# Column products with standing weights and joined high and low inputs in a hybrid encoder block

## The chip, the cores and the metric

The kernel runs on one core of one Trainium2 chip. The metric is the device time of one execution in microseconds (us). Of the kernel before, three runs gave a median of 793.23 us (792.94 to 793.36). The profile is that of one further execution; its times count from the start of its span.

The engines are called as in the profile: PE (TensorE: products; PEld is its loading of weights), DVE (VectorE), ACT (ScalarE), POOL (GpSimd) and SP (SyncE, whose queue starts the weights' transfers).

## The reference

One layer of an encoder on x of 256 tokens by 1024 features, in float32. Five residual parts follow one another:

```python
x = x + 0.5 * rmsnorm(swiglu(rmsnorm(x), w_in, w_down))      # FFN 1, width 2816
h = rmsnorm(x)
q_a, f_a, i_a, g_a, q_b, k_b, v_b, f_b, gates = split(h @ w_in)
A = hgrn2_chunkwise(q_a, f_a, i_a)      # gated linear recurrence, 8 heads of 128
B = fox_attention(q_b, k_b, v_b, f_b)   # causal attention with forget gates
y = sigmoid(gate_A) * (A @ w_branch_a) + sigmoid(gate_B) * (B @ w_branch_b)
x = x + rmsnorm(y @ w_out)
x = x + rmsnorm(mem_cross_attention(rmsnorm(x), rmsnorm(mem)))   # 4 heads, 256 memory rows
x = x + 0.5 * rmsnorm(swiglu(rmsnorm(x), w_in2, w_down2))    # FFN 2
```

with `swiglu(h) = (silu(gate) * up) @ w_down`, where `gate` and `up` are the two halves of `h @ w_in`, and `rmsnorm` dividing each token by the root of its mean square. The kernel applies that per-token factor (`rstd`) after the product, and the gain of each feature before it.

## The kernel before, in words

**Numbers in two parts.** A float32 number is split into a high part that TensorE takes in one pass (`F32R`) and the low rest. A product is three: high by high, high by low, low by high, summed in PSUM. Weights come as units of 512 KB, [128 x 1024], through SP's queue into `raw` (four buffers); ACT casts `hi` (L142) and DVE subtracts to `lo` (L144), eight buffers each. A `chunk` (L153) is four units: 1024 rows of 512 columns, in eight blocks `kb` of 128 rows.

**Two forms of projection.** `proj_tok` (L184): 128 tokens stand in the array and the weights move, 512 columns wide; 24 products for each half of the tokens. The result has tokens on the partitions. `proj_col` and `proj_col2` (L193, L202): a 128x128 block of weights stands and the 256 tokens move, 24 products of 256 for 128 columns: weight high by input high, the same by input low, weight low by input high. The result has features on the partitions, which is what a following product needs. The inputs lie in a `Pair` (L166), with high and low parts in different tiles.

**The feed-forwards** (`ffn`, L352) run over 11 chunks of 256 gate and 256 up columns. A chunk is done in token form (`act_tok`, L382): two halves, each with Silu on ACT (L372, with the token's factor as a scale) and the product with `up` on DVE (L377). For the down product its result has to have features on the partitions: `flush` (L358) issues four transposes on PE (L367) behind a given product, and splits their result (L162, L163). `down` (L401) then adds the chunk's 24 products of 512 columns to four accumulators. The first chunks go differently: in the first feed-forward chunks 0 to 2 walk through both token halves at once (`act_first`, L387), as the inputs arrive; in the second, chunks 0 and 1 are taken half by half while the residual before is finished (`second_half`, L418). The down products trail the chunks by one or two; the last three chunks (`STAG`) are left to the end, where `post` (L310) or `post_last` (L325) normalises the sum and adds it to `xs`: squares summed on ACT (L250), the product with the gain on DVE (L317, L340), the factor from `rstd_of` (L227).

**Around the change.** The per-token factors as a row over all partitions come from `row_of` (L270): DVE transposes, a POOL transfer to DRAM, and a POOL transfer back to all partitions (L275, L277). Forget gates (L575 to L588) and the recurrence's queries (L589 to L599) are column products, then multiplied by that row (L581, L596). Memory queries (L1047 to L1053) are column products that `split` brings into high and low. They are followed by the memory values (`mem_v`) and the scores (`mem_scores`, L1071). `half` (L524) transposes the new `xs` for the next part's input.

**The order** is that of the program, with two changes: `after(i)` gives a group priority behind the i-th product that was issued (constants such as `L_ACT`), and the scheduler of the framework moves instructions of an engine where it expects an operand later. PSUM has eight banks: four `acc`, two `mm`, two `tr`.

Of the kernel before, what the change touches and what calls it, by code (L numbers as in the profile page):

```python
# [18 lines left out]
P = 128  # L19
# [16 lines left out]
L_ACT = 21  # L36
L_LAST = 8
L_F1 = 24
# [41 lines left out]
def block_kernel(ctx: ExitStack, tc: tile.TileContext, wts, head_in, gf_in, x_in, mem_in, memT_in, cols, rows, fbias, masks, out):  # L80
# [85 lines left out]
    class Pair:  # L166
# [14 lines left out]
        def lo(self, kb, a=0, b=T):  # L181
            return self.l[kb // 4][:, kb % 4, a:b]

    def proj_tok(ps, X, units, h, n=512):  # L184
# [63 lines left out]

    def ssq(dst, src):
        S.activation(junk[:, : src.shape[-1]], src, AF.Square, accum_out=dst)  # L250

# [7 lines left out]

    fac = [cp.tile([P, 64], F32, name=nm("fac")) for _ in range(2)]  # L260
    for t in fac:
# [47 lines left out]

    def post(ps, h, grow, factor=1.0, store=False):  # L310

        s = s1(2, name="ss2")
        ts = []
        for j in range(2):
            ssq(s[:, j : j + 1], ps[j])
            t = sp.tile([P, 512], F32, tag="z2", name=nm("post"), bufs=3)
            V.scalar_tensor_tensor(out=t, in0=ps[j], scalar=-factor * SC_RSTD, in1=grow[:, j * 512 : (j + 1) * 512], op0=ALU.mult, op1=ALU.mult)  # L317
            ts.append(t)
        r = rstd_of(s, scaled=False)
        for j, (t, xh) in enumerate(zip(ts, x_halves(h))):  # L320
            V.scalar_tensor_tensor(out=xh, in0=t, scalar=r, in1=xh, op0=ALU.mult, op1=ALU.add)
            if store:
                nc.sync.dma_start(out[h * P : (h + 1) * P, j * 512 : (j + 1) * 512], xh)

    def post_last(ps, h, grow, factor):  # L325

        s = s1(2, name="ss2")
        ts = []
        for j in range(2):
            ssq(s[:, j : j + 1], ps[j])  # L330
# [9 lines left out]
            V.scalar_tensor_tensor(out=t, in0=ps[j], scalar=-factor * 16.0, in1=grow[:, j * 512 : (j + 1) * 512], op0=ALU.mult, op1=ALU.mult)  # L340
            ts.append(t)
# [9 lines left out]

    def ffn(w_in, w_dn, X, r2, n_tok, i_row, first_half, second_half=None):  # L352

        acts = {}
# [15 lines left out]
        def act_evac(ps, c, h):  # L370
            sg = sp.tile([P, FC], F32, tag="c1", name=nm("sg"), bufs=7)
            silu = S.activation(sg, ps[:, :FC], AF.Silu, scale=r2[h])  # L372
            if c == NFF - 1 and h == 1 and not first_half:
                with tc.issue_after(silu.ins):
                    S.activation(warm, ones[:, 0:1], AF.Abs_reciprocal_sqrt)
            a = sp.tile([P, FC], F32, tag="c1", name=nm("at"), bufs=7)
            V.scalar_tensor_tensor(out=a, in0=ps[:, FC:], scalar=r2[h], in1=sg, op0=ALU.mult, op1=ALU.mult)  # L377
            ats[c, h] = a
            if h == 1:
                late.append(c)  # L380

        def act_tok(c, h):  # L382
            ps = mm()
            proj_tok(ps, X, chunk(w_in, c), h)
            act_evac(ps, c, h)

        def act_first(cs, bank):  # L387
# [25 lines left out]
        for h in range(2):  # L413
            m = len(log)
            for c in range(n_tok):
                act_tok(c, h)
            if h == 0 and n_tok:
                second_half(m)  # L418
        accs = None
        done = 0  # L420
        if callable(r2):
            outs = act_first((0, 1), acc)
            r2 = r2()
            for c in range(2):
                acts[c] = m4([P, 2, 2, T], F32R, "act")
# [3 lines left out]
        for c in range(n_tok, NFF):  # L429
# [28 lines left out]
        for cut in (left, right):  # L458
            for c in range(NFF - STAG, NFF):
                if c == NFF - 1 and cut == left:  # L460
                    flush(m + L_LAST)
                down(c, 0, (cut,))
        post(accs[0], 0, grow, 0.5, not first_half)
        m = len(log)
        if first_half:
            for c in range(NFF - STAG, NFF):
                down(c, 1)
            first_half(m)
            post(accs[1], 1, grow, 0.5)
        else:  # L470
            for cut in (left, right):
                for c in range(NFF - STAG, NFF):
                    down(c, 1, (cut,))
            post_last(accs[1], 1, grow, 0.5)

    X1 = Pair()
    heads, raw1 = [], []  # L480
# [31 lines left out]
    def norm_1():  # L512
# [6 lines left out]
        return [rstd_x(x_halves(h)) for h in range(2)]  # L519

    X2 = Pair()
    r2 = [None, None]
# [46 lines left out]

    def halves(ps):  # L570
        return ps.rearrange("p h (b t) -> p h b t", b=2)
# [17 lines left out]
    for c in range(2):  # L589
        u = chunk("q_a", c)  # L590
        q = m4([P, 2, 4, P], n="q")
        for j in range(2):
            qj = heads_of(q, j)
            ps = proj_col2(X2, u, (2 * j, 2 * j + 1))
            z = sp.tile([P, 2, 2, P], F32, tag="z2", name=nm("z2"), bufs=3)
            V.tensor_tensor(out=z, in0=halves(ps), in1=bc(row2h, [P, 2, 2, P], 1), op=ALU.mult)  # L596
            S.activation(qj, z, AF.Sigmoid)
# [420 lines left out]

    X3 = Pair()
    r3 = [None, None]  # L1020
# [111 lines left out]
    for kb in range(4):  # L1132
        behind.extend(marks[kb // 2])
        unit("mo", kb)
        behind.clear()
    X4 = Pair()
    r4 = [None, None]
# [8 lines left out]
    rows_proj(po[1], AO, "mo", 1, range(3, KB))  # L1146
    half(X4, r4, 0, G_F2, m + L_MO)
    post(po[1], 1, g3)


    def second(m):
        half(X4, r4, 1, G_F2, m + L_F2)

# [92 lines left out]
```

## Time and profile before

| | |
|---|---|
| median of three runs | 793.23 us |
| lowest and highest | 792.94, 793.36 us |
| the profiled execution | 791.78 us |
| its span | 790.0 us |
| its granted TensorE clock | 0.998 |
| weights and other data moved | 147.82 MB, mean 187 GB/s |
| PE instructions in the span | 4736 products and transposes |
| transposes of flushes (L367) | 22 x 4 |

How to read the profile's lines. In the page's list of busy times, each engine has its busy time, its share of the span and its number of instructions. A line of a group gives the line of the source, the engine, the operation, output and inputs by tile name, the shapes and the count, then the busy time and the mean duration of one in ns, then the time that the engine was idle just before and what ended it. A line of a timeline begins with its start and its duration. Products on PE overlap in the record: the time of one in a row of many is the distance between starts. A line of windows has, for each engine, the busy time in a stretch and the number of instructions.

### The profile page before, as it was taken

Reading aid. Unit: us, or ns where it says so; the run is one execution under the profiler, and the core shown is the slowest. Engines: PE = TensorE matmul, PEld = TensorE weight load, DVE = VectorE, ACT = ScalarE, POOL = GpSimd, SP = SyncE. Lnnn points to the kernel's source line nnn. Section 1 sums busy time; section 2 is a strip of 40 time slices with the busy share of each in tenths; the row PEclk is TensorE's granted clock in tenths of the full one; section 3 lists DMA queues with packets and bytes.
Section 4 is the critical chain, followed back from the end, with each engine's and each line's share of the span. In section 5 each row is a group of like instructions: output and inputs, shape, how many; then the busy total and the mean of one; then the engine's idle time right before and its main releaser. Section 6 shows DMA issues by size and latency. Waiting matters only on the chain.

```text
span 790.0 us, 12203 instructions
## 1 busy us (share of the span) xinstructions
PE 782.3 (99%) x4736; PEld 677.4 (86%) x4736; DVE 519.0 (66%) x825; ACT 426.8 (54%) x656; POOL 13.7 (2%) x36
## 2 busy tenths in 40 slices
PE   9999999999999999999999999999999999999996
PEld 7888888888899999998788888999888888888885
DVE  6774545557767899488686666964669754545543
ACT  7654444546664677357774345643657644434541
POOL 0000000000000102100000000000000000000000
PEclk9999999999999999999999999999999999999999
DMA  9786654563654547634576654555263655554521
GB/s 347 247 271 205 228 189 160 188 202 118 210 196 144 180 136 224 258 120 152 197 251 222 211 191 160 164 186 181 65 229 134 227 199 209 203 200 161 183 84 54
DMA packets 44345, 147.82 MB, mean 187 GB/s; under 512 B 5048, under 2 KB 8768, under 8 KB 44288
## 3 DMA queue, kind: packets, MB, share of 16 engines
q1 hardware_dynamic: 43168, 144.83, 53.9%
q0 software_dynamic: 688, 1.85, 1.0%
q8 instruction: 37, 0.61, 0.3%
q10 hardware_dynamic: 432, 0.37, 0.1%
q14 instruction: 20, 0.16, 0.1%
HBM read 145.97 MB, written 1.06 MB: 186 GB/s over the span
## 4 chain that ended last, share of the span: by engine, by line
PE 98%; DMA 1%; DVE 0%; ACT 0%; SPq 0%; issue 0%; DVEq 0%; ACTq 0%
PE mm L94 68%; PE acc L94 27%; PE tr L367 1%; PE tr L94 1%; PE tr L294 1%; DMA head<-in_head_dram 1%; PE tr L898 0%; PE tr L989 0%; PE acc L1099 0%; DVE xs L348 0%; DVE post L340 0%; ACT hi L507 0%; SPq L491 0%; ACT hT L285 0%; SPq L486 0%
## 5 line engine op out<-in xcount | busy, mean ns | idle before, releaser
L144 DVE TENSOR_TENSOR lo<-raw,hi 128x1024 fp32r<-128x1024 f32 (+1 forms) x256 | 306.7, 1206 | 122.4 <-ACT hi L142 114.3
L142 ACT CAST hi<-raw 128x1024 fp32r<-128x1024 f32 (+1 forms) x256 | 262.4, 1038 | 149.3 <-PE mm L94 83.3
L94 PE MATMUL mm<-lo,hT 128*128 128x512 f32 (+1 forms) x592 | 226.9, 385 | 0.0
L94 PE MATMUL mm<-hi,hT 128*128 128x512 f32 (+1 forms) x592 | 226.8, 385 | 0.0
L94 PE MATMUL mm<-hi,lT 128*128 128x512 f32 (+1 forms) x592 | 226.5, 385 | 0.0
L94 PEld LDWEIGHTS mm<-hi,lT 128*128 128x128 f32 x592 | 111.2, 188 | 21.4 <-DVE lT L286 0.2
L94 PEld LDWEIGHTS mm<-hi,hT 128*128 128x128 f32 x592 | 111.2, 188 | 21.4 <-ACT hT L285 0.3
L94 PEld LDWEIGHTS mm<-lo,hT 128*128 128x128 f32 x592 | 111.0, 188 | 20.7
L94 PE MATMUL acc<-hi,act 128*128 128x512 f32 x352 | 111.8, 390 | 0.0
L94 PE MATMUL mm<-hT,lo 128*128 128x256 f32 x384 | 109.0, 284 | 0.0
L94 PE MATMUL mm<-hT,hi 128*128 128x256 f32 x384 | 108.9, 284 | 0.0
L94 PE MATMUL mm<-lT,hi 128*128 128x256 f32 x384 | 108.8, 283 | 0.0
L94 PEld LDWEIGHTS acc<-hi,act 128*128 128x128 f32 x352 | 66.0, 188 | 13.6 <-DVE act L163 0.4
L94 PEld LDWEIGHTS mm<-hT,hi 128*128 128x128 f32 x384 | 73.6, 192 | 0.1
L94 PEld LDWEIGHTS mm<-lT,hi 128*128 128x128 f32 x384 | 73.6, 192 | 0.1
L94 PEld LDWEIGHTS mm<-hT,lo 128*128 128x128 f32 x384 | 73.6, 192 | 0.1
L94 PE MATMUL acc<-lo,act 128*128 128x512 f32 x176 | 69.7, 398 | 0.0
L372 ACT ACTIVATE sg<-mm,rstd 128x256 f32<-128x256 f32 x40 | 19.0, 475 | 75.8 <-PE mm L94 75.8
L377 DVE SCALAR_TENSOR_TENSOR at<-mm,rstd,sg 128x256 f32<-128x256 f32 x40 | 19.2, 481 | 57.4 <-ACT sg L372 57.4
L94 PEld LDWEIGHTS acc<-lo,act 128*128 128x128 f32 x176 | 33.1, 188 | 6.1
L94 PE MATMUL acc<-hi,hT 128*128 128x512 f32 x96 | 35.0, 392 | 0.5 <-ACT hi L507 0.4
L94 PE MATMUL acc<-hi,lT 128*128 128x512 f32 x96 | 35.1, 393 | 0.0
(198 smaller groups left out, 655.7 us busy)
## 6 DMA issues: line engine op xcount, KB each, us to landing
raw<-in_wts_dram SPq DMA_DIRECT2D x247, 512.0 KB, 4.4
raw<-in_gf_dram SPq DMA_DIRECT2D x12, 344.0 KB, 3.8
head<-in_head_dram SPq DMA_DIRECT2D x7, 392.0 KB, 6.6
grow<-in_rows_dram SPq DMA_DIRECT2D x4, 512.0 KB, 6.1
xs<-in_x_dram SPq DMA_DIRECT2D x2, 512.0 KB, 7.8
cbm<-cd POOLq DMA_DIRECT2D x2, 512.0 KB, 9.0
brow<-in_rows_dram SPq DMA_DIRECT2D x4, 256.0 KB, 4.6
memT<-in_memT_dram SPq DMA_DIRECT2D x2, 512.0 KB, 5.4
```

Of the source, the lines that this page charges most:

```text
L94: log.append(PE.matmul(*args, **kw).ins)
L142: S.copy(h, r)
L144: V.tensor_tensor(out=l, in0=r, in1=h.bitcast(F32), op=ALU.subtract)
L294: PE.transpose(ps[:, j * P : (j + 1) * P], src(kb), ident)
L367: PE.transpose(trv[:, j, h * P : (h + 1) * P], ats[c, h][:, j * P : (j + 1) * P], ident)
L372: silu = S.activation(sg, ps[:, :FC], AF.Silu, scale=r2[h])
L377: V.scalar_tensor_tensor(out=a, in0=ps[:, FC:], scalar=r2[h], in1=sg, op0=ALU.mult, op1=ALU.mult)
```

## The change

Inputs of four projections (X1 to X4) are held in `Joined` tiles, in which the high and the low part of a block lie side by side, 256 + 256 columns. `proj_both` computes a block of 128 columns with standing weights: eight products of the high weights with both input parts at once (512 moving columns), then eight of the low weights with the high part (256). The left half of the bank then holds two of the three sums, the right half the third. `added` copies the right half out of PSUM on ACT and adds on DVE.

The feed-forward chunks from the fourth (first feed-forward) and the third (second) on are done by `act_col` in that form: two gate blocks, the token's factor by a row, Silu, two up blocks, the product, the split. No transposes follow. The row is made by `row_of` once per feed-forward. `up` keeps its missing factor, which comes into `post` and `post_last` as an operand (`pre`). The down products of chunk 7 now stand behind chunk 10's `act_col`. Forget gates, the recurrence's queries and the memory queries take `proj_both`, each block in a bank of `acc`. `k_b`, `q_b` and the memory keys keep `proj_col2`.

```diff
+    class Joined:
+        def __init__(self):
+            self.t = [m4([P, 2, 2, T], F32R, "hlT") for _ in range(KB // 2)]
...
+        def both(self, kb):
+            return self.t[kb // 2][:, kb % 2].rearrange("p s t -> p (s t)")
+
+    def proj_both(ps, X, units, cb):
+        a, b = cb * P, cb * P + P
+        for part in range(2):
+            for kb in range(KB):
+                w = blk(units, kb)[part][:, a:b]
+                if part:
+                    MM(ps[:, :T], w, X.hi(kb), start=False, stop=(kb == KB - 1))
+                else:
+                    MM(ps, w, X.both(kb), start=(kb == 0), stop=False)
+
+    def added(out, ps):
+        two = len(out.shape) == 3
+        lo = sp.tile([P, T], F32, tag="c1", name=nm("plo"), bufs=7)
+        S.copy(lo, ps[:, T:])
+        a, b = (t.rearrange("p (b t) -> p b t", b=2) if two else t for t in (ps[:, :T], lo))
+        V.tensor_tensor(out=out, in0=a, in1=b, op=ALU.add)
...
-    def ssq(dst, src):
-        S.activation(junk[:, : src.shape[-1]], src, AF.Square, accum_out=dst)
+    def ssq(dst, src, scale=1.0):
+        S.activation(junk[:, : src.shape[-1]], src, AF.Square, scale=scale, accum_out=dst)
...
-            V.scalar_tensor_tensor(out=a, in0=ps[:, FC:], scalar=r2[h], in1=sg, op0=ALU.mult, op1=ALU.mult)
+            V.tensor_tensor(out=a, in0=ps[:, FC:], in1=sg, op=ALU.mult)
...
+        def act_col(c):
+            u = chunk(w_in, c)
+            gate, up = (sp.tile([P, 2, T], F32, tag="z2", name=nm(n), bufs=3) for n in ("gate", "up"))
+            for j in range(2):
+                ps = mm()
+                proj_both(ps, X, u, j)
+                added(gate[:, j], ps)
+            V.tensor_tensor(out=gate, in0=gate, in1=bc(row, [P, 2, T], 1), op=ALU.mult)
+            silu = S.activation(gate, gate, AF.Silu)
...
+            for j in range(2):
+                ps = trp() if c > 2 else acc()
+                proj_both(ps, X, u, 2 + j)
+                added(up[:, j], ps)
+            V.tensor_tensor(out=up, in0=up, in1=gate, op=ALU.mult)
+            split(acts[c][:, 0], acts[c][:, 1], up)
...
-                for h in range(2):
-                    n = len(log)
-                    act_tok(c, h)
-                    if c == 2 or c > NFF - STAG + 1 and h == 0:
-                        flush(n + L_ACT)
+                n = len(log)
+                act_col(c)
+                flush(n + L_ACT)
+                flush(n + L_ACT + 20)
...
-            while done < min(c - 1, NFF - STAG):
+            while done < (NFF - STAG if c == NFF - 1 else min(c - 1, NFF - STAG - 1)):
...
-            ps = proj_col2(X2, u, (2 * j, 2 * j + 1))
-            V.tensor_tensor(out=fj, in0=halves(ps), in1=bc(row2h, [P, 2, 2, P], 1), op=ALU.mult)
+            for i in (2 * j, 2 * j + 1):
+                ps = acc()
+                proj_both(ps, X2, u, i)
+                added(f[:, :, i], ps)
+            V.tensor_tensor(out=fj, in0=fj, in1=bc(row2h, [P, 2, 2, P], 1), op=ALU.mult)
...
-        for j in range(2):
-            js = slice(2 * j, 2 * j + 2)
-            ps = proj_col2(X3, u, (2 * j, 2 * j + 1))
-            split(QM.h[c][:, js], QM.l[c][:, js], ps)
+        for i in range(4):
+            ps = acc()
+            proj_both(ps, X3, u, i)
+            hi, lo = QM.h[c][:, i], QM.l[c][:, i]
+            S.copy(hi, ps[:, :T])
+            t = sp.tile([P, T], F32, tag="c1", name=nm("qm"), bufs=7)
+            V.tensor_tensor(out=t, in0=ps[:, :T], in1=hi.bitcast(F32), op=ALU.subtract)
+            V.tensor_tensor(out=lo, in0=ps[:, T:], in1=t, op=ALU.add)
```

The queries of the recurrence change as the forget gates do. `row = row_of(fac[3])` stands behind the second half of the second feed-forward's input, `row = row_of(fac[2])` behind the first one's norms.

More of the change, by code (lines that the diff above doesn't have):

```diff
@@ L36 @@
 L_ACT = 21
-L_LAST = 8
 L_F1 = 24
@@ L257, in rstd_x @@
         return rstd_of(s, into=into)
-    fac = [cp.tile([P, 64], F32, name=nm("fac")) for _ in range(2)]
+    fac = [cp.tile([P, 64], F32, name=nm("fac")) for _ in range(4)]
     for t in fac:
@@ L308, in load_row, with post @@
         return r
-    def post(ps, h, grow, factor=1.0, store=False):
+    def post(ps, h, grow, factor=1.0, store=False, pre=None):
+        f, sc = times(pre, -factor * SC_RSTD)
         s = s1(2, name="ss2")
@@ L323, in post, with post_last @@
                 nc.sync.dma_start(out[h * P : (h + 1) * P, j * 512 : (j + 1) * 512], xh)
-    def post_last(ps, h, grow, factor):
+    def post_last(ps, h, grow, factor, pre):
+        f, sc = times(pre, -factor * 16.0)
         s = s1(2, name="ss2")
@@ L339, in post_last @@
             t = sp.tile([P, 512], F32, tag="z2", name=nm("post"), bufs=3)
-            V.scalar_tensor_tensor(out=t, in0=ps[j], scalar=-factor * 16.0, in1=grow[:, j * 512 : (j + 1) * 512], op0=ALU.mult, op1=ALU.mult)
+            V.scalar_tensor_tensor(out=t, in0=ps[j], scalar=f, in1=grow[:, j * 512 : (j + 1) * 512], op0=ALU.mult, op1=ALU.mult)
             ts.append(t)
@@ L371, in act_evac @@
             sg = sp.tile([P, FC], F32, tag="c1", name=nm("sg"), bufs=7)
[L372 to L375, printed above, removed]
+            S.activation(sg, ps[:, :FC], AF.Silu, scale=r2[h])
             a = sp.tile([P, FC], F32, tag="c1", name=nm("at"), bufs=7)
-            V.scalar_tensor_tensor(out=a, in0=ps[:, FC:], scalar=r2[h], in1=sg, op0=ALU.mult, op1=ALU.mult)
+            V.tensor_tensor(out=a, in0=ps[:, FC:], in1=sg, op=ALU.mult)
             ats[c, h] = a
@@ L385, in act_tok @@
             act_evac(ps, c, h)
+        def act_col(c):
[7 more added lines that the diff above has]
+            silu = S.activation(gate, gate, AF.Silu)
+            if c == NFF - 1 and not first_half:
+                with tc.issue_after(silu.ins):
+                    S.activation(warm, ones[:, 0:1], AF.Abs_reciprocal_sqrt)
+            for j in range(2):
[4 more added lines that the diff above has]
+            split(acts[c][:, 0], acts[c][:, 1], up)
         def act_first(cs, bank):
@@ L418, in ffn @@
                 second_half(m)
+                row = row_of(fac[3])
         accs = None
@@ L423, in ffn @@
             r2 = r2()
+            row = row_of(fac[2])
             for c in range(2):
@@ L459, in ffn @@
             for c in range(NFF - STAG, NFF):
-                if c == NFF - 1 and cut == left:
-                    flush(m + L_LAST)
                 down(c, 0, (cut,))
-        post(accs[0], 0, grow, 0.5, not first_half)
+        post(accs[0], 0, grow, 0.5, not first_half, r2[0])
         m = len(log)
@@ L468, in ffn @@
             first_half(m)
-            post(accs[1], 1, grow, 0.5)
+            post(accs[1], 1, grow, 0.5, pre=r2[1])
         else:
@@ L473, in ffn @@
                     down(c, 1, (cut,))
-            post_last(accs[1], 1, grow, 0.5)
-    X1 = Pair()
+            post_last(accs[1], 1, grow, 0.5, r2[1])
+    X1 = Joined()
     heads, raw1 = [], []
```

37 lines of the change are left out of this document (24 added, 13 removed).

## The prediction

> **What bounds the kernel now.** I read first the busy times and the chain that ended last, then the largest groups of instructions.
>
> ```profile
> span 790.0 us, 12203 instructions
> ...
> PE 782.3 (99%) x4736; PEld 677.4 (86%) x4736; DVE 519.0 (66%) x825; ACT 426.8 (54%) x656; POOL 13.7 (2%) x36
> ...
> PE 98%; DMA 1%; DVE 0%; ACT 0%; SPq 0%; issue 0%; DVEq 0%; ACTq 0%
> ...
> L144 DVE TENSOR_TENSOR lo<-raw,hi 128x1024 fp32r<-128x1024 f32 (+1 forms) x256 | 306.7, 1206 | 122.4 <-ACT hi L142 114.3
> L142 ACT CAST hi<-raw 128x1024 fp32r<-128x1024 f32 (+1 forms) x256 | 262.4, 1038 | 149.3 <-PE mm L94 83.3
> ```
>
> TensorE is 98% of the chain. VectorE and ScalarE spend over half of their busy time on splitting weights, and ScalarE's idle time there ends by a matmul: the splits wait for weight buffers that PE gives back. So two things count: what PE is given, and whether the new order lets the other engines deliver in time. The profiled execution took 791.78 us (span 790.0); the median of the three runs is 793.23, 1.45 above.
>
> **The price of a product.** The timeline of PE in a stretch of token products, at the start of the column products, and behind their end:
>
> ```profile
> 46.27 0.39 PE L94 MATMUL mm<-hi,hT 128*128 128x512 f32 x1
> ...
> 55.56 0.39 PE L94 MATMUL mm<-hi,lT 128*128 128x512 f32 x1
> ```
>
> ```profile
> 213.84 0.28 PE L94 MATMUL mm<-hT,hi 128*128 128x256 f32 x1
> ```
>
> ```profile
> 259.91 0.32 PE L94 MATMUL mm<-hi,hT 128*128 128x344 f32 x1
> ```
>
> From the first to the second row are 41 products: 9.29 / 41 = 0.2266 us for one of 512 columns. From the third to the fourth are 384 products of 256: 46.07 / 384 = 0.1200. (The 0.39 and 0.28 are durations that overlap; only the distance between starts counts.) The difference is 0.1066 for 256 columns, so 0.0134 is paid per product whatever its width. That is what one wide product in place of two narrow ones saves.
>
> **Transposes.** A flush is four transposes between products:
>
> ```profile
> 38.06 0.60 PE L367 MATMUL tr<-ident,at 128*128 128x128 f32 x4
> 38.41 0.71 PE L94 MATMUL mm<-lo,hT 128*128 128x512 f32 x2
> 38.96 0.40 PE L94 MATMUL acc<-hi,act 128*128 128x512 f32 x1
> ```
>
> From 38.06 to 38.96 stand two products and the flush: 0.90 - 2 x 0.2266 = 0.45 us. A whole steady chunk says the same (VectorE's L377 of two successive chunks, and the busy times of the stretch between):
>
> ```profile
> 101.47 0.48 DVE L377 SCALAR_TENSOR_TENSOR at<-mm,rstd,sg 128x256 f32<-128x256 f32 x1 [3.66 <-ACT sg L372]
> ...
> 118.25 0.48 DVE L377 SCALAR_TENSOR_TENSOR at<-mm,rstd,sg 128x256 f32<-128x256 f32 x1 [3.63 <-ACT sg L372]
> ```
>
> ```profile
> 101.02:117.80 16.78, 16.78 (x78) 13.90 (x77) 8.83 (x9) 7.64 (x10) 0.00 (x0) 1.00 0.55 189
> ```
>
> The period is 16.78; 48 + 24 products of 512 are 72 x 0.2266 = 16.31; 0.47 is left for the flush. I take 0.465.
>
> **The change part by part.**
>
> 1. *Feed-forward chunks* (3 to 10 of the first, 2 to 10 of the second, 17 in all). Gate and up were 48 products of 512, 10.88 us. Now four blocks of 8 wide and 8 narrow: 32 x 0.2266 + 32 x 0.1200 = 11.09. So +0.21 each, **+3.6 us**: the token form was already wide throughout, and 16 more products pay 0.0134 each.
>
> 2. *Their transposes* go, 17 flushes of 0.465: **-7.9 us**. Five flushes stay (chunks 0 to 2 and 0 to 1).
>
> 3. *Forget gates, recurrence and memory queries*: 24 blocks, each 24 products of 256 (2.88 us) before, 8 of 512 and 8 of 256 (2.77) after. -0.107 x 24 = **-2.6 us**. The sum on PE is **-6.9 us**.
>
> By the Trainium skill, "TensorE: Matmul & The Clock Gate", section "Back-to-back issue gap", the warm spacing of lone matmuls is columns / 2.4 plus 2.5 ns, 216 and 109 ns at 512 and 256. Parts 1 and 3 would then be estimated at +0.7 and -0.5, and the sum at -7.7; the rows above, 227 and 120, decide here.
>
> 4. *Other engines in a chunk.* Prices, from the groups with shapes apart:
>
> ```profile
> L144 DVE TENSOR_TENSOR lo<-raw,hi 128x1024 fp32r<-128x1024 f32 x244 | 296.4, 1223 | 117.6 <-ACT hi L142 109.7
> ...
> L94 PEld LDWEIGHTS mm<-hT,lo 128*128 128x128 f32 x384 | 73.6, 192 | 0.1
> ...
> L377 DVE SCALAR_TENSOR_TENSOR at<-mm,rstd,sg 128x256 f32<-128x256 f32 x40 | 19.2, 481 | 57.4 <-ACT sg L372 57.4
> L372 ACT ACTIVATE sg<-mm,rstd 128x256 f32<-128x256 f32 x40 | 19.0, 475 | 75.8 <-PE mm L94 75.8
> ...
> L285 ACT ACTIVATE hT<-tr,cols_s 128x128 fp32r<-128x128 f32 x64 | 21.5, 367 | 9.8 <-DVE lT L286 8.7 <-PE tr L294 0.6
> L250 ACT ACTIVATE junk<-acc 128x512 f32<-128x512 f32 x20 | 12.0, 598 | 27.6 <-PE acc L94 27.5
> L317 DVE SCALAR_TENSOR_TENSOR post<-acc,grow 128x512 f32<-128x512 f32 x14 | 9.7, 690 | 17.8 <-ACT junk L250 17.8
> L948 DVE SCALAR_TENSOR_TENSOR zg<-mm,fac,brow 128x512 f32<-128x512 f32 x8 | 6.0, 748 | 2.7 <-PE mm L94 2.7
> L703 DVE TENSOR_TENSOR k<-k,tq 128x512 f32<-128x512 f32 x6 | 4.1, 684 | 0.0
> L802 DVE SCALAR_TENSOR_TENSOR k_b<-mm,row 128x256 f32<-128x256 f32 x8 | 3.0, 415 | 1.9 <-PE mm L94 1.9
> L1063 ACT ACTIVATE hT<-mm,fac 128x512 fp32r<-128x512 f32 x4 | 2.8, 694 | 13.9 <-PE mm L94 13.9
> L597 ACT ACTIVATE q<-z 128x512 f32<-128x512 f32 x4 | 2.5, 633 | 8.6 <-DVE z L596 8.6
> ```
>
> ScalarE loses two Silu of 256 (0.95) and gets one of 512 (0.63, as L597) and four copies of 128x256 out of PSUM. No row has that copy; it lies between L285 (0.37) and L372 (0.475), and I take 0.46, L372's shape: +1.5. VectorE loses two L377 (0.96) and gets four adds (0.415, as L802) and two multiplies of 512 (0.684): +2.1. So ScalarE has some 9.2 us and VectorE 10.9 of a chunk of 16.52 (16.78 - 0.47 + 0.21). Throughput covers both.
>
> 5. *When weights come free.* A token chunk walks through the contraction twice, and its first unit of weights is free after 24 + 6 products, 6.8 us into 10.9. A column chunk walks through it four times, wide before narrow: the first `hi` is free at 3 x 2.77 + 2 x 0.2266 = 8.8 us, the first `lo` at 10.4, the last at 11.1. With eight buffers of each kind the third and fourth unit of the next chunk wait for these. VectorE's two splits behind 10.4 end at about 11.6 and 12.8 (1.22 each, L144); PE reaches the next chunk at 11.09 + 24 x 0.2266 = 16.5. **Slack 3.7 us**, so I cost it at nothing; the down products hide it, and a unit later than that stalls PE by the excess in each of 17 chunks.
>
> 6. *Per-token factors.* `up` is left unscaled and the squares and products behind it take a factor from memory: +0.09 (L1063 against L250) and +0.06 (L948 against L317). Only at the very end is nothing beside it, since VectorE's last product there waits for the squares:
>
> ```profile
> 784.39 0.69 DVE L340 SCALAR_TENSOR_TENSOR post<-acc,grow 128x512 f32<-128x512 f32 x1 [3.33 <-ACT junk L250]
> ```
>
> So **+0.15 us**. The factor's way into a row is two DMAs on POOL's queue, twice more:
>
> ```profile
> 418.06 0.63 POOL L275 DMA_DIRECT2D rd<-runs  x1 [96.16 <-DVE runs L273]
> 423.57 0.56 POOL L277 DMA_DIRECT2D row<-rd  x1 [4.88 <-DMA rd<-runs]
> ```
>
> ```profile
> row<-rd POOLq DMA_DIRECT2D x2, 128.0 KB, 6.2
> ```
>
> ```profile
> 610.83 0.14 DVE L246 TENSOR_SCALAR rstd<-y 128x1 f32<-128x1 f32 x1
> ```
>
> ```profile
> 620.48 0.47 ACT L372 ACTIVATE sg<-mm,rstd 128x256 f32<-128x256 f32 x1 [0.45 <-PE mm L94]
> ```
>
> In the second feed-forward the factor is ready at 610.97. VectorE turns it after one weight split, near 613.8; 5.5 + 6.2 later, 625.5, the row is there. The last token half ends at 620.48, two gate blocks are 5.55 us, so it is wanted at about 626.4, and PE has the up blocks and a chunk's down products before anything depends on it: nothing, with some 4 us to spare. In the first, norms are long done. POOL's queue has nothing else near either (13.7 us of work in all).
>
> 7. *Moved steps.* Chunk 7's down products go behind chunk 10's gate and up, with their two weight units in SP's queue, so three chunks' worth need not wait for the last flush: the cover that chunk 10's split needs is there (its split ends about 2 us before its down products start). At the first feed-forward's end VectorE has one more weight split ahead of these updates:
>
> ```profile
> 186.23 1.41 DVE L321 SCALAR_TENSOR_TENSOR xs<-post,y,xs 128x512 f32<-128x512 f32 x2
> ```
>
> ```profile
> 187.78 1.03 PE L294 MATMUL tr<-ident,xs 128*128 128x128 f32 x8
> ```
>
> They end 0.14 us before the transposes that need them. A split is 1.22; the transposes move back by two or three products (0.45 to 0.68): between nothing and 0.8, I take **+0.3**. At the second one's start the first down products stand behind activations that now queue behind the first blocks' copies and adds: between nothing and 1.2 (a copy, an add and a token Silu more), **+0.4**.
>
> 8. *Evacuation of q, f and memory queries.* Each block has a bank to itself, two PSUM reads and, for the gates and q, the factor on SBUF. The last q comes a copy and an add later than before (0.9), twice that where two blocks queue (1.8); the order of the changed kernel has some 15 to 30 products of 344 columns ahead of the recurrence's, which I estimate at 2.3 to 5 us (0.12 and 0.23 on both sides of their width). The memory scores' last operands wait for VectorE in the order of the changed program, with two weight splits and two sums ahead: between nothing and 1.0, **+0.25**.
>
> Sum: -6.9 + 0.15 + 0.3 + 0.4 + 0.25 = **-5.8 us**: 786.0 for the profiled execution, **787.4** as a median.
>
> **The rivals.**
>
> (A) *Transitions cost more*: all the upper ends together, 0.15 + 0.8 + 1.2 + 1.0 = 3.2, plus up to 2 us of the recurrence's start if its 2.3 us are used up: -3.7 to -1.7, 789.5 to 791.5. For: VectorE is full around the recurrence. Against: PE has products of other parts to put in between.
>
> (B) *Slower: weights are held until the chunk's end.* Place: each new chunk, part 5. VectorE's splits come when it also has adds, multiplies and the split of the activations. It decides from 3.7 us of delay; beyond it every 0.35 us per chunk takes 17 x 0.35 = 6 us, the whole gain. Delays of 4.7 us give -5.8 + 17 = +11, about 804. For: ScalarE's idle time already ends with PE's releases, 83.3 us of it. Against: both engines are idle for a third of the chunk.
>
> (C) *Narrow products with new weights each cost their load.* 0.192 in place of 0.120 for 17 x 32 + 24 x 8 = 736 products: +53 us, 840. Against: 384 products with a load of 0.192 each came every 0.120 us. By the Trainium skill, "TensorE: Matmul & The Clock Gate", section "The mechanism", a load overlaps running matmuls only when its row group differs; by that rule loads of the full array would show, and those 384 rows don't bear it out.
>
> (D) *No stall shows at all*: -6.9, 786.3; and down to 785.0, if the steady flush is dearer elsewhere than in the two places above (0.08 more for each of 17).
>
> (E) *The wide products aren't wide*: the moving side is not one run of 512, and each block is 24 products of 256: the chunks then cost 17 x (96 x 0.1200 - 10.88) = +10.9 in place of +3.6 and the blocks nothing, so +4.1 with the stalls, 797. Against: the order of the changed kernel has products of 128x512 on the joined tiles.
>
> **How the numbers follow.** Forecast 0.62, A 0.16, B 0.08, C 0.01, D 0.12, E 0.01. Forecast and D together span 785.0 to 789.5 (0.74); A reaches to 791.5, and with all of it but its end, some 0.86 lie in **785.0 to 791.0**. A measurement of this kernel can tell about 0.2% (1.6 us) from no change. Faster (below 791.6) is the forecast, D and A less 0.03 for A's end: 0.87; the same is that 0.03 and the mild part of B, 0.03: 0.06; slower is the rest of B, 0.05, with C and E: 0.07.
>
> **What would show it.** A chunk's period of 16.5 us; no transposes behind the third chunk; products of the f, q and memory-query blocks 0.2266 and 0.120 apart, 2.77 per block; PE's idle time before L94 not above 2 us in all. Wrong would be: a period above 16.8, idle time of PE ended by `hi` or `lo` in the feed-forwards (B), a wide product not 0.227 or a narrow one not 0.120 apart (C, E), or several us of idle time at the transitions (A).

## The result and the profile after

In the first comparison the changed kernel took 789.31 us in the median (788.61 to 790.77, six runs), the kernel before 792.52 (791.88 to 793.36); the ratio is 0.9963 with an interval of 0.9952 to 0.9973. Beside the experiments it ran twice more: 790.17 against 791.87 (ratio 0.9973, 0.9962 to 0.9984) and 789.54 against 791.80 (0.9974, 0.9962 to 0.9985). So the change saves 0.26 to 0.37% by these ratios, 2 to 3 us (1.7 to 3.2 by the medians). 787.4 was forecast, within 785.0 to 791.0; the direction held, and 2 to 3 of the 5.8 us came.

The page of the profile after, busy times, chain and the largest groups of the splits and of the new copy:

```profile
span 787.5 us, 12412 instructions
...
PE 777.8 (99%) x4748; PEld 674.8 (86%) x4748; DVE 556.4 (71%) x927; ACT 447.4 (57%) x727; POOL 15.9 (2%) x42
...
PE 94%; DVE 3%; DMA 1%; issue 1%; ACT 1%; DVEq 0%; ACTq 0%
...
L143 DVE TENSOR_TENSOR lo<-raw,hi 128x1024 fp32r<-128x1024 f32 (+1 forms) x256 | 304.7, 1203 | 80.2 <-ACT hi L141 55.3
L141 ACT CAST hi<-raw 128x1024 fp32r<-128x1024 f32 (+1 forms) x256 | 258.8, 1037 | 93.1 <-PE mm L93 46.3
...
L213 ACT COPY plo<-mm 128x256 f32<-128x256 f32 x34 | 12.5, 372 | 48.1 <-PE mm L93 48.1
```

PE has 12 products and transposes more and is busy 4.5 us less. Five flushes are left, as forecast. DVE has 37 us more and ACT 21, and both have less idle time ahead of the splits. The chain holds 3% of DVE now, where it held none. The view of the waits (engine and line, released by; us, times, longest) says where PE stood still, after and, as the second fence, before:

```profile
PE tr L93 <- PEq L1303: 0.8, 1, 0.8
PE mm L93 <- DVE lo L143: 0.8, 1, 0.8
PE acc L93 <- ACT hi L568: 0.5, 1, 0.5
PE tr L93 <- ACT hT L1131: 0.4, 1, 0.4
PE tr L335 <- DVE hlT L327: 0.2, 1, 0.2
```

```profile
PE tr L94 <- PEq L1235: 0.8, 1, 0.8
PE acc L94 <- ACT hi L507: 0.4, 1, 0.4
```

Three waits are new, each of one time only: on a low part of a weight, on a memory value, and, at the third input's transposes, on a joined tile that DVE writes:

```profile
503.75 0.66 PE L335 MATMUL tr<-ident,xs 128*128 128x128 f32 x4 [0.15 <-DVE hlT L327]
```

No chunk of a feed-forward waits. (The view counts idle time from the end of the product ahead. Products in a row start 0.23 us apart and each is recorded as 0.39 long, so PE loses more than the view says: the low part's 0.8 is 0.95 from start to start, with 0.1 more at the next product.)

**The price of a change of width.** The timeline of PE in the two gate blocks of a steady chunk (start, duration, count):

```profile
61.05 1.98 PE L93 MATMUL mm<-hlT,hi 128*128 128x512 f32 x8
62.86 1.11 PE L93 MATMUL mm<-hlT,lo 128*128 128x256 f32 x8
63.81 2.00 PE L93 MATMUL mm<-hlT,hi 128*128 128x512 f32 x8
65.65 1.11 PE L93 MATMUL mm<-hlT,lo 128*128 128x256 f32 x8
66.61 0.40 PE L93 MATMUL tr<-hlT,hi 128*128 128x512 f32 x1
```

The first eight wide products follow wide ones (the down products) and take 62.86 - 61.05 = 1.81 = 8 x 0.2266. The next eight follow narrow ones and take 1.84. In the trace's starts these eight are 233, 236, 228, 233, 231, 226, 227 and 227 ns apart, 28 ns over the steady price; the first narrow product behind a wide one takes 113 in place of 120, the second 119. So each change to narrow and back costs some 0.02 us. Each of the 92 new blocks holds one such change. It was to be seen before: there a run of wide products behind narrow ones begins

```profile
549.19 0.40 PE L94 MATMUL mm<-lo,hT 128*128 128x512 f32 x1
549.42 0.40 PE L94 MATMUL mm<-hi,lT 128*128 128x512 f32 x1
549.66 0.39 PE L94 MATMUL mm<-hi,hT 128*128 128x512 f32 x1
549.89 0.40 PE L94 MATMUL mm<-lo,hT 128*128 128x512 f32 x1
550.12 0.39 PE L94 MATMUL mm<-hi,lT 128*128 128x512 f32 x1
```

at distances of 0.23, 0.24, 0.23 and 0.23, where 0.2266 is steady; in the trace's starts the first five are 28 ns over it, in a kernel without a joined tile.

**The chunk.** Starts of the first gate product of two successive chunks on PE's timeline before:

```profile
61.68 0.40 PE L94 MATMUL mm<-hi,hT 128*128 128x512 f32 x1
...
78.48 0.39 PE L94 MATMUL mm<-hi,hT 128*128 128x512 f32 x1
```

And after, the one that follows 61.05:

```profile
77.66 0.39 PE L93 MATMUL mm<-hlT,hi 128*128 128x512 f32 x1
```

16.80 became 16.61, where 16.52 was forecast. In it the other engines are busy as follows (PE, PEld, DVE, ACT, POOL, each with its count):

```profile
61.05:77.66 16.61, 16.61 (x89) 14.34 (x88) 10.49 (x14) 8.54 (x13) 0.00 (x0) 1.00 0.58 186
```

DVE 10.49 and ACT 8.54 (forecast 10.9 and 9.2; the copy took 0.37 and not 0.46).

**Stages.** For all comparisons below the trace is cut at starts on PE: the fourth chunk of the first feed-forward, the transposes behind it, the forget gates, the output gates (the 344-wide products), attention's last products, the memory scores' transposes, the two inputs of the second feed-forward, the last product, and the end of the span. Times in us, each from the profiled execution of its kernel; "after" three times:

```
stage                     before   after (three)          joined  blocks  ffn
start to fourth chunk      40.39   39.77  41.55  40.64     40.27   41.31   41.94
feed-forward 1            142.90  141.81 141.81 141.81    142.90  142.93  141.81
its end, first input       26.06   27.06  27.03  27.06     26.76   26.76   27.02
forget gates, q            46.07   44.67  44.67  44.67     46.07   44.67   46.07
gates to attention        135.54  135.76 135.80 135.96    135.64  135.60  135.54
to memory scores          162.84  162.48 162.50 162.50    163.17  162.50  163.23
memory read                36.37   36.89  36.36  36.56     36.35   36.36   36.36
input of feed-forward 2    12.98   13.15  13.15  13.15     13.15   12.99   13.17
feed-forward 2            175.55  173.96 173.96 173.96    175.45  175.53  173.92
behind the last product     6.80    7.31   7.33   7.31      6.78    6.79    7.31
sum without the start     745.10  743.10 742.61 742.98    746.26  744.14  744.44
```

Most stages repeat to 0.05 us, the stage from the gates to attention to 0.2, the memory read to 0.5. The start doesn't: it lies between 39.8 and 41.9 without regard to the kernel (the last section says why). So the sums without the start leave out the largest source of scatter: by them the change saves 2.0 to 2.5 us. They stand for one execution each, and the kernel before has only one.

### The profile page after: what moved, and what is told of

Read it like the earlier page. It is cut to its first block, busy times and chain, and to the rows that moved or that the text cites. A ratio compares the mean times of both kernels' runs of the same rounds, so it can differ in the third digit from the quotient of the medians.

```text
span 787.5 us, 12412 instructions
## 1 busy us (share of the span) xinstructions
PE 777.8 (99%) x4748; PEld 674.8 (86%) x4748; DVE 556.4 (71%) x927; ACT 447.4 (57%) x727; POOL 15.9 (2%) x42
## 4 chain that ended last, share of the span: by engine, by line
PE 94%; DVE 3%; DMA 1%; issue 1%; ACT 1%; DVEq 0%; ACTq 0%
PE mm L93 45%; PE acc L93 36%; PE tr L93 12%; PE tr L335 1%; DVE lo L143 1%; DMA raw<-in_wts_dram 1%; DMA head<-in_head_dram 0%; PE tr L962 0%; ACT junk L283 0%; DVE lT L162 0%; DVE xs L363 0%; PE tr L412 0%; DVE post L359 0%; PE tr L1053 0%; DVE hlT L327 0%
## 5 line engine op out<-in xcount | busy, mean ns | idle before, releaser
L93 PE MATMUL mm<-hi,hlT 128*128 128x512 f32 (+1 forms) x448 | 132.8, 378 | 0.0
L93 PE MATMUL mm<-hlT,hi 128*128 128x512 f32 (+1 forms) x528 | 114.7, 339 | 0.0
L93 PEld LDWEIGHTS mm<-hlT,hi 128*128 128x128 f32 x528 | 89.7, 190 | 9.6
L93 PEld LDWEIGHTS mm<-hi,hlT 128*128 128x128 f32 x448 | 82.1, 188 | 14.4 <-DVE hlT L327 0.6
L93 PE MATMUL mm<-lo,hlT 128*128 128x512 f32 (+1 forms) x224 | 83.1, 378 | 0.8 <-DVE lo L143 0.8
L93 PE MATMUL mm<-hlT,lo 128*128 128x256 f32 x400 | 74.5, 283 | 0.0
L93 PEld LDWEIGHTS mm<-hlT,lo 128*128 128x128 f32 x400 | 61.7, 191 | 2.8
L93 PE MATMUL tr<-hlT,hi 128*128 128x512 f32 x256 | 64.1, 392 | 0.0
L93 PEld LDWEIGHTS tr<-hlT,hi 128*128 128x128 f32 x256 | 46.0, 189 | 8.2
L93 PE MATMUL acc<-hlT,hi 128*128 128x512 f32 x208 | 52.0, 392 | 0.0
L93 PEld LDWEIGHTS mm<-lo,hlT 128*128 128x128 f32 x224 | 41.9, 188 | 7.8 <-DVE lo L143 1.2
```

The costliest lines, as they stand in the source:

```text
L93: log.append(PE.matmul(*args, **kw).ins)
```

## The experiments

The two theories, set out from this trace: (1) changes of width cost PE time, beside waits at the seams; (2) products keep their steady prices, and all that is missing are waits.

**One part alone: the 24 blocks.** The kernel before, with joined tiles and `proj_both` for the forget gates, q and the memory queries only:

```diff
-    X2 = Pair()
+    X2 = Joined()
...
-            ps = proj_col2(X2, u, (2 * j, 2 * j + 1))
+            for i in (2 * j, 2 * j + 1):
+                ps = acc()
+                proj_both(ps, X2, u, i)
+                added(f[:, :, i], ps)
```

> Only the forget gates, the recurrence's queries and the memory queries take the joined products (24 blocks); the feed-forwards stay in token form with their transposes. Theory 1 (each change from narrow to wide products costs 28 ns over the next wide ones, of which the first narrow one gives 8 back): a block 2.79 us, 24 x -0.088 = -2.1, less 0.3 to 0.5 for a wait at the memory scores, so about -1.7 against before. Theory 2 (products at their steady prices, all losses are waits at the seams between stages): a block 2.77 us, -2.6, and the waits at the seams to be seen as idle time of PE.

Measured 790.96 against 792.01, ratio 0.9987 (0.9979 to 0.9995): -1.05, and -0.96 by the stages. The 16 blocks of forget gates and q took 44.67, 2.79 each, as theory 1 has it. But the first input's stage cost 0.70 more, though the feed-forward ahead of it was untouched; neither theory had that.

**The other part alone: the feed-forwards**, with `proj_col2` for the 24 blocks.

> Only the feed-forward chunks take the joined products; the other 24 blocks stay narrow. Theory 1: a chunk's period is 16.61 us (three changes from narrow to wide in it and one into the down products), 17 x -0.19 = -3.2, and the waits at the seams (0.95 at the first input projection behind the first feed-forward, 0.3 at its transposes, 0.15 at the end) leave about -1.7. Theory 2: period 16.53 and -4.3, less the same waits: -2.9. If the two parts are independent, their gains add up to that of the whole change, about -3.2.

Measured 791.12 against 792.01, ratio 0.9993 (0.9982 to 1.0004), not to be told from nothing; by the stages -0.66. The feed-forward's stages are those of the whole change to 0.04 us. Here too the first input's stage (+0.96) and the memory part (+0.39) cost more than their products can. The parts don't add up to the whole (-1.6 against -2.0 to -2.5): both hold joined tiles for X2 and X3, and the next run shows what these cost.

**The joined tiles alone.** The kernel before with this, and no other product or operation:

```diff
-    X1 = Pair()
+    X1 = Joined()
```

and so for X2, X3 and X4.

> The kernel before with the joined tiles for X1 to X4 and nothing else: the same products, the same transposes, the same work on every engine. Theory 1 (the joined tiles by themselves change the order in which VectorE's queue is written, so that the residual update stands ahead of the weight splits): the stage from the first transposes to the forget gates takes 0.7 us more than before, the memory part 0.4 and the second feed-forward's input 0.2, in all +1.2 against before. Theory 2 (these waits come of the additional work on ScalarE and VectorE): no difference to before, 0 within 0.2 us.

Measured 793.27 against 791.87, ratio 1.0014 (1.0005 to 1.0022); by the stages +1.16, in the three places that were named: +0.70, +0.33, +0.17. Of these 0.70 + 0.33 = 1.03 are in both runs of a part; counted once, the two parts give -2.65. DVE's timeline at the first input, before and then with the joined tiles:

```profile
193.57 1.23 DVE L144 TENSOR_TENSOR lo<-raw,hi 128x1024 fp32r<-128x1024 f32 x1
...
194.78 1.22 DVE L144 TENSOR_TENSOR lo<-raw,hi 128x1024 fp32r<-128x1024 f32 x1
...
196.04 1.22 DVE L144 TENSOR_TENSOR lo<-raw,hi 128x1024 fp32r<-128x1024 f32 x1
...
197.24 1.22 DVE L144 TENSOR_TENSOR lo<-raw,hi 128x1024 fp32r<-128x1024 f32 x1
...
199.02 1.42 DVE L321 SCALAR_TENSOR_TENSOR xs<-post,y,xs 128x512 f32<-128x512 f32 x2
```

```profile
195.07 1.23 DVE L144 TENSOR_TENSOR lo<-raw,hi 128x1024 fp32r<-128x1024 f32 x1
196.21 1.41 DVE L336 SCALAR_TENSOR_TENSOR xs<-post,y,xs 128x512 f32<-128x512 f32 x2
197.54 3.49 DVE L144 TENSOR_TENSOR lo<-raw,hi 128x1024 fp32r<-128x1024 f32 x3
```

Before, four weight splits stand ahead of the residual update (`xs`); with joined tiles the update goes in behind the first. PE needs the second split first, and waits:

```profile
198.81 0.50 PE L94 MATMUL mm<-lo,hlT 128*128 128x512 f32 x1 [0.37 <-DVE lo L144]
```

From start to start this product comes 0.76 behind the one ahead and the next 0.34, in place of 0.23 each: 0.64 of the 0.70. The work on DVE is the same; the scheduler wrote its queue in another order. What in the joined tile makes it do so, no run shows. The third input's 0.33 is the wait on `hlT` shown above, which stands in this run's view of the waits too; the fourth's 0.17 was not followed up.

**The order put back.** The changed kernel, with the loads of that projection ahead in the program and the update held behind the last of its splits:

```diff
+            with tc.issue_after(last) if last is not None else nullcontext():
                 V.scalar_tensor_tensor(out=xh, in0=t, scalar=r, in1=xh, op0=ALU.mult, op1=ALU.add)
...
+    def first(m):
+        half(X2, r2, 0, G_MIX, m + L_F1, into=fac_of(0, 0))
+        chunk("i_a", 0)
+        behind.extend(evicted)
+        chunk("i_a", 1)
+        behind.clear()
```

> The changed kernel, with VectorE's queue at the end of the first feed-forward put back into the order of before: the four weight splits of the input projection's second chunk ahead of the residual update of the second token half. Theory 1: the wait of 0.95 us on a low part goes, the stage from the first transposes to the forget gates is 26.1 to 26.3 as before, -0.8 to -1.0 against the changed kernel. Theory 2 (the weights arrive late there for want of buffers): the wait stays, and the update comes later in addition: 0 to +0.5.

The stage took 26.23 in place of 27.06: -0.83, theory 1. DVE's timeline has the four splits in one run ahead of the update again, and the wait is gone:

```profile
194.85 4.63 DVE L144 TENSOR_TENSOR lo<-raw,hi 128x1024 fp32r<-128x1024 f32 x4
199.40 1.41 DVE L365 SCALAR_TENSOR_TENSOR xs<-post,y,xs 128x512 f32<-128x512 f32 x2
```

Time 789.77 against 791.87 (ratio 0.9964, 0.9951 to 0.9977), the changed kernel beside it 790.17. The whole shows less than the stage: the sum of the stages is 742.44, 0.2 to 0.7 below the changed kernel's, mainly because the gates to attention took 136.08 in this execution; and the medians differ by less than their spread.

**Wide and narrow by turns.** The changed kernel with sixteen changes of width in each block:

```diff
-        for part in range(2):
-            for kb in range(KB):
-                w = blk(units, kb)[part][:, a:b]
...
+        for kb in range(KB):
+            wh, wl = blk(units, kb)
+            MM(ps, wh[:, a:b], X.both(kb), start=(kb == 0), stop=False)
+            MM(ps[:, :T], wl[:, a:b], X.hi(kb), start=False, stop=(kb == KB - 1))
```

> As the changed kernel, but within a block each wide product is followed at once by the narrow one of the same rows, in place of eight wide and then eight narrow ones. Theory 1 in its mild form (the loss is spread over the five wide products behind a change: 6, 9, 1, 6, 4 ns, and only the first of them is ever reached here, while each narrow one comes 7 ns early): a pair is 0.233 + 0.113 = 0.346, a block 2.77, 92 blocks x -0.025 = -2.3, about 787. Theory 1 in its hard form (each change costs its 20 ns whole): a block 2.93, +13 us, about 802. Theory 2: no change of the products' prices; weights come free a little earlier: 0 to -1.

Measured 792.93 against 792.01, ratio 1.0009 (1.0001 to 1.0018); the sum of the stages is 745.96, 3.1 above the changed kernel's mean of 742.9: the whole gain and more. Neither form of theory 1 was right in size. PE's timeline:

```profile
71.21 0.40 PE L93 MATMUL tr<-hlT,hi 128*128 128x512 f32 x1
71.45 0.28 PE L93 MATMUL tr<-hlT,lo 128*128 128x256 f32 x1
71.57 0.40 PE L93 MATMUL tr<-hlT,hi 128*128 128x512 f32 x1
71.81 0.28 PE L93 MATMUL tr<-hlT,lo 128*128 128x256 f32 x1
71.92 0.40 PE L93 MATMUL tr<-hlT,hi 128*128 128x512 f32 x1
72.15 0.28 PE L93 MATMUL tr<-hlT,lo 128*128 128x256 f32 x1
72.27 0.40 PE L93 MATMUL tr<-hlT,hi 128*128 128x512 f32 x1
```

Three pairs from 71.21 to 72.27 are 0.353 each, 0.347 at steady prices: 0.0065 for each pair, and 92 x 8 x 0.0065 = 4.8 in place of 92 x 0.02 = 1.8. The difference, 3.0, is what was measured, and it lies where the blocks are: 1.1 for the 32 of the first feed-forward, 1.1 for the 36 of the second, 0.54 for 16 and 0.3 for 8. So "wide ones first" is worth 3 us here. A new bank of PSUM can't be the reason: here each pair pays inside one bank.

**Half as many changes.** In the feed-forward chunks, two blocks at once: 16 wide, then 16 narrow.

```diff
+    def proj_pair(pss, X, units, cbs):
+        for part in range(2):
+            for ps, cb in zip(pss, cbs):
+                a, b = cb * P, cb * P + P
+                for kb in range(KB):
...
-                ps = mm()
-                proj_both(ps, X, u, j)
-                added(gate[:, j], ps)
+            pss = [mm(), mm()]
+            proj_pair(pss, X, u, (0, 1))
+            for j in range(2):
+                added(gate[:, j], pss[j])
```

> As the changed kernel, but in the feed-forward chunks two blocks are done together, 16 wide products and then 16 narrow ones, so that a chunk has two changes from narrow to wide in place of four. Theory 1: 17 x 2 x -0.02 = -0.7 us, a period of 16.57. Theory 2: no change of the period; it may grow, as the first gate block is read out later.

On PE's timeline a chunk starts at

```profile
61.59 0.39 PE L93 MATMUL mm<-hlT,hi 128*128 128x512 f32 x1
```

and the next at

```profile
78.17 0.39 PE L93 MATMUL mm<-hlT,hi 128*128 128x512 f32 x1
```

so the period is 16.58 (theory 1: 16.57). The first feed-forward's stage fell from 141.81 to 141.47. The second rose to 174.34: its first chunk's later evacuation made the down products wait 0.6 for activations. 790.86 against 792.01, ratio 0.9980 (0.9971 to 0.9989). The sum of the stages, 743.31, is no better than the changed kernel's: the price came out as forecast, the gain didn't.

**Both mended.** DVE's order, and pairs from the fourth chunk on only, which spares that wait; run twice.

> The changed kernel with that order and with two blocks done together in the feed-forward chunks from the fourth on (16 wide products, then 16 narrow ones). The two gains add up if they are independent: -0.9 for the order and 16 x 2 x -0.02 = -0.6 for the halved number of changes from narrow to wide, so -1.5 against the changed kernel and -3.5 to -4.4 against before. If the later evacuation costs as much as the fewer changes bring, only -0.9.

> The version with pairs and VectorE's order once more, for its interval: stages as before within 0.1 us but for the first 40 us; -3 to -4 against the kernel before, -1.2 to -1.6 against the changed one.

789.05 against 791.87 (ratio 0.9958, 0.9945 to 0.9972), then 789.15 against 791.80 (0.9968, 0.9956 to 0.9979). Stages: 141.49 for the first feed-forward, 26.2 for the first input, 173.6 to 173.7 for the second feed-forward; sums without the start 741.07 and 741.70, 1.2 to 1.8 below the changed kernel's mean of 742.9 and 3.4 to 4.0 below the kernel before. It is the best of all by the sums, but both of its profiled executions were the fastest of their six (787.82 and 788.28). By the medians it beats the kernel before clearly, and the changed one, which ran on the same two chips at 790.17 and 789.54, by 1.1 and 0.4 us only: there the intervals overlap, so that it is the faster of the two is not shown.

**A quarter of the changes.** All four blocks of a chunk at once, 32 wide and 32 narrow.

> The kernel with VectorE's order put right, and in the feed-forward chunks from the fourth on all four blocks done together, 32 wide products and then 32 narrow ones: one change from narrow to wide in a chunk, in place of two with pairs and four in the changed kernel. Theory 1: the period of a chunk falls from 16.61 by 0.04 to 0.05 for pairs, as measured, and by another 0.02 here: 16.55, the first feed-forward's stage 141.3 and the second's 173.4, -0.3 against pairs. Rival: the four banks are read out only at the chunk's end, and the splits of the next chunk's weights queue behind that: waits of PE in each chunk, slower than pairs.

788.58 against 791.80 (ratio 0.9960, 0.9947 to 0.9974), but the sum of the stages is 743.03, 1.3 to 2.0 above pairs. Sums and medians disagree here (by the medians it is 0.6 below the pairs beside it, with overlapping intervals), so which of the two is faster stays open. The steady period is 16.55 from PE's starts (61.31 to 77.86), as theory 1 has it; both feed-forwards lost more than that, at their first or last new chunks. At the second one's start the down products wait for the activations of the first chunks:

```profile
636.63 0.50 PE L93 MATMUL acc<-hi,act 128*128 128x512 f32 x1 [0.67 <-ACT act L162]
```

The rival had the reason (a late evacuation; and once, at 631.97, a weight that waited for its cast), though not in every chunk. And where one wide run goes through four banks, its products stay 227 ns apart across each change of bank.

**The changed kernel again**, beside the runs of the last two groups:

> The changed kernel once more, beside the next three on one chip. From the sum of its stages (all but the start): -2.0 us against before, of which the first 40 us may add or take 1 to 2 by when the full clock is granted. Stage by stage within 0.1 us of the first profile, but for the first 40 us.

> The changed kernel beside these two on one chip: -2.0 to -2.6 against before by the sum of its stages without the first 40 us.

The table above has its stages: -2.5 and -2.1 by the sums, and but for the memory read (0.5 and 0.3) and the gates to attention (up to 0.2) the stages came within 0.1 us of the first profile's. The second run of the pairs had the same exception, the memory read, and its gain over the changed kernel beside it was 1.3 by the sums and 0.4 by the medians (1.2 to 1.6 expected).

## Why the prediction came out as it did

*Part 1, the chunks, and part 2, their transposes.* Forecast -0.25 a chunk, measured -0.19: 17 x 0.06 = 1.0 of the gain was not there. The four changes of width cost 0.08 a chunk (0.02 each), and 0.02 of that came back because the flush was a little dearer than 0.465: 16.80 - 72 x 0.2266 = 0.48. **The step that failed is "0.0134 is paid per product whatever its width"**, with a sum made of the two steady prices.

*Part 3, the 24 blocks.* 2.79 and not 2.77: -1.40 for 16 (forecast -1.71), and for the eight memory queries -0.67 to -0.73 (162.50 against 163.17 and 163.23; forecast -0.86). Together with the chunks the products gave about -5.3 in place of -6.9.

*Part 4 and part 5, the other engines and the weights.* Right: no feed-forward chunk waited for a weight, so that rival (B) didn't come.

*Part 6, the factors.* The row of the second feed-forward came in time. At the very end the last update ends 4.07 us behind the last product's start and 3.94 before, +0.13 as forecast:

```profile
780.18 0.39 PE L93 MATMUL acc<-hi,act 128*128 128x512 f32 x1
...
782.58 1.67 DVE L391 SCALAR_TENSOR_TENSOR xs<-post,y,xs 128x320 f32<-128x320 f32 x4
```

(780.18 to 784.25; before 783.18 to 787.12.) Another 0.37 lies behind it, in every kernel with the new feed-forwards and in no other. The trace places it between two of POOL's closing instructions (0.41 idle, from 786.89 to 787.30; before 0.04); why POOL stands there, no run told.

*Part 7, the moved steps.* Forecast +0.3 at the first feed-forward's end and +0.4 at the second's start. At the first, 0.43 came (the stage fell by 1.09 where eight chunks give 1.52): the transposes stood 0.25 late and one product later. At the second it was 0.12 (1.59 of 1.71). But what cost most was not named, and was put at nothing: the stage behind the first end, where the residual update stands ahead of the weight splits, took +1.0, and 0.8 of it went when the order was put back. The joined tile alone brings 0.70 of the +1.0, without more load on DVE; the other 0.3 comes with the new feed-forwards (27.02 in their run, 26.76 with tiles alone), and what of them does it was not tried. The same tiles cost 0.33 and 0.17 at the third and fourth inputs, +1.2 in all. The order of the changed kernel's DVE queue shows the first of these by itself; the prediction followed that order to the transposes, and not to the weights of the stage behind them.

*Part 8, evacuation.* The memory scores' 0.25 came out as nothing to 0.5, from one execution to the next, and at another operand (a memory value whose evacuation stands behind a cast that waits for its transfer). From the output gates to attention, where nothing was forecast, 0.2 to 0.4 were lost; which wait does it was not tried.

*The rivals.* What happened lies between the forecast and (A): the seams cost 2.8 to 3.3 us (5.3 less the 2.0 to 2.5 that came), where 1.1 was forecast; 1.7 to 1.9 of it is in places that neither named (the first input +1.0, the tiles at the third and fourth +0.5, the gates to attention 0.2 to 0.4), and another 1.6 went to a price that no rival had. (C) is refuted again: in a run of eight, narrow products with new weights each came 0.113, 0.119 and then 0.120 apart. So is (E): the wide ones are 128x512 and 0.2266 apart. Two of the signs set ahead were not met: the period is 16.61 and not 16.5, and PE's idle time ahead of its products is 2.5 us in the view of the waits (1.2 before), where at most 2 was set.

*Luck in the number.* The time lies in the stated range in part because the kernel before ran faster than the 793.23 from which the range was counted: 792.52, and 791.80 to 792.01 in the later comparisons. By the difference, 2 to 3 us, the result belongs to (A), which had 1.7 to 3.7, and not to the forecast's 3.7 and more.

## What to carry to other kernels

A price taken from a long run of equal products doesn't hold at its edges: where products of two widths alternate, measure the first few behind each change, and group them. And a change of where operands lie can cost a good part of what its arithmetic saves (here 1.2 of 5.3 us), because the scheduler writes the queues anew: compare each engine's order for a whole stage behind every edit, and not only at the instruction that moved.

## What the runs showed of the hardware

*The surcharge behind a change of width* hardly depended on how many narrow products stood ahead: in the changed kernel's first profile it is 28 ns behind runs of 4, 8, 16, 24 and 53 of them and 25 behind a single one, spread over five wide products. One run of six, behind the transposes of a flush, shows 16.

*The start.* The first products ran 0.427 us apart in 7 of the 13 profiled executions, for 2 to 5 us; in an eighth only the first was slow, and in the other five they ran at 0.23. In the run with the feed-forwards alone ten products go from 4.81 to 9.25; in the changed kernel's first profile six go from 4.62 to 6.21:

```profile
4.81 2.07 PE L93 MATMUL acc<-hi,hlT 128*128 128x512 f32 x4 [0.70 <-ACT hi L568]
6.69 1.05 PE L93 MATMUL acc<-lo,hlT 128*128 128x512 f32 x2
7.54 1.91 PE L93 MATMUL acc<-hi,hlT 128*128 128x512 f32 x4
9.25 0.88 PE L93 MATMUL acc<-lo,hlT 128*128 128x512 f32 x2
```

```profile
4.62 1.20 PE L93 MATMUL acc<-hi,hlT 128*128 128x512 f32 x4 [0.51 <-ACT hi L568]
5.66 0.71 PE L93 MATMUL acc<-lo,hlT 128*128 128x512 f32 x2
6.21 1.07 PE L93 MATMUL acc<-hi,hlT 128*128 128x512 f32 x4
```

The windows' view seems to contradict it; in the first of these two starts it gives a granted clock of 1.00 (the column behind POOL's):

```profile
4.80:9.60 4.80, 4.79 (x11) 3.80 (x12) 3.70 (x8) 3.31 (x7) 0.00 (x0) 1.00 1.03 401
```

But the view counts time without a record as full speed. The trace's first record of the granted clock begins at 9.80 in that execution, and at 3.9 to 9.3 in the others; where products stand ahead of it they are 0.427 apart (the first two 0.59), and those behind it 0.23. By the Trainium skill, "TensorE: Matmul & The Clock Gate", section "Back-to-back issue gap", a cold array takes columns / 1.2 ns, 427 for 512: the trace agrees, with 426 to 428 ns from start to start. Without slow products the stage of the start took 39.8 to 40.4 us, with nine to eleven of them 41.6 to 41.9. So what comes and goes here from one execution to the next moves the time by up to 2 us, as much as the whole change.
